# An encoder block on one core: row-summed modulation, gate A in the first stage, norms between units, y stored from ScalarE's queue

## The chip, the core and the metric

One core of a Trainium2 chip runs one launch. The metric is the device time in microseconds (us). Five engines work each in its own order: TensorE (PE: matmuls and transposes into PSUM banks), VectorE (DVE), ScalarE (ACT), GpSimd (POOL) and SyncE (SP, which here only issues DMAs). An instruction waits on semaphores for others; what stands behind it on its engine waits too. DMAs issued by SP or by ScalarE move data between HBM and SBUF.

## The reference

512 tokens, width 2048, float32. What matters here:

```python
c_act = silu(c)
mod = c_act @ w_ada + b_ada                    # w_ada is 2048 x 12288
sh1, sc1, g1, sh2, sc2, g2 = split(mod, 6)
h = rms_norm(x, norm1_w) * (1 + sc1) + sh1
qa, ka, va, qb, kb, vb, ga, gb = split(h @ w_in)   # 1024, 256, 256, 3 x 1024, 2 x 2048 columns
ya = global_gqa(rope(rms_norm(qa)), rope(rms_norm(ka)), va)     # 8 heads, 2 kv heads
yb = neighbourhood_attention(qb, kb, vb, rpb)                   # 8 heads
merged = sigmoid(ga) * (ya @ w_oa) + sigmoid(gb) * (yb @ w_ob)
x = x + g1 * (merged @ w_out)
h2 = rms_norm(x, norm2_w) * (1 + sc2) + sh2
x = x + g2 * ((silu(h2 @ w_gate) * (h2 @ w_up)) @ w_down)
out = rms_norm(x, final_w)
```

## The kernel before

Every product is done in three float32r matmuls: each operand is split into a high part (ScalarE, L114, `whi`, `h3h`) and a low part (L115, `wlo`, `h3l`; VectorE, or POOL where the helper gets `eng=G`), and `mm3` multiplies high by high, high by low, low by high. A *unit* is one weight tile of 128 x 1024 (512 KB): loaded by SP into a `raw` buffer (four of them), split into `whi` and `wlo` (three of each), and used by 24 matmuls of 512 columns.

The stages, in order of time:

- *First stage* (L299 to L396). x comes in as four token tiles; each gets its row scale, is scaled, and is transposed by TensorE into `xnT`. Then nine slices of k (one or two of the sixteen 128-wide parts of the width): `ada1` makes scale `s1` and shift `t1` for the slice, ScalarE makes h from `xnT` (L351), POOL splits h and all weights, and TensorE accumulates kv (all k in four `mm` banks), the first half of q and one of gate A's four groups (`g_acc`, 512 columns) in pieces that VectorE adds up (L391).
- *Modulation.* `ada_mod` loads rows of `w_ada` for a few columns, multiplies them by silu(c) of that row and adds them up over sixteen k on VectorE (`acc`, L255 and L257); TensorE sums over the partitions by a matmul against a column of ones (L275, bank `Y`, raised in priority), and VectorE finishes s and t (L263 to L265). `ada_gate` does the same for the gates g1 and g2.
- *Norm and attention A.* `norm_rope` (L422) norms and rotates k and then q (L450 to L455) and transposes them (L437); heads 0 to 3, q's second half (`form2`), gate A's rest (`gates`), q's second norm and heads 4 to 7 follow. `keep_y` (L463) stores each head's y to HBM by SP's queue.
- *Attention B* (L570 on): per half v, then per pair of heads q and k, then `att_b`. Behind each unit `pump` runs one step of the background list `bg`: scale and shift of the second norm, later the gates g1 and g2.
- *Gate B* (L583), then the loads and splits of y (L595), the merge (`w_oa`, `w_ob`), `w_out`, the feed-forward part and the last norm.

A scheduler sets each engine's order from the program, buffers and priorities; pools that are released give their space to the next, whose first writers wait for the old users.

Of the kernel before, what the change touches and what calls it, by code (L numbers as in the profile page):

```python
# [17 lines left out]
P = 128  # L18
D = 2048
# [61 lines left out]
def encoder_block(ctx: ExitStack, tc, xp, c, w_ada, b_ada, norm1_w, w_in, q_norm_w, k_norm_w, tb,  # L81
# [22 lines left out]
    const.tile([P, 32], F32, name="left_edge")  # L104
# [36 lines left out]
    later = []  # L141

# [28 lines left out]
    def form2(w, c0, xs, evac, r0=0, eng=V, tiles=range(NT)):  # L171

        n = len(xs)
        banks = {i: bank("mm") for i in tiles}
        for k0 in range(0, n, 2):
            m = min(2, n - k0)
            hi, lo = wsplit(w, r0 + k0, m, c0, 512, eng)
            for kk in range(m):
                xh, xl = xs[k0 + kk]
                for i in tiles:  # L180
                    sl = slice(i * P, (i + 1) * P)
                    mm3(banks[i], xh[:, sl], xl[:, sl], hi[:, kk], lo[:, kk], k0 + kk == 0, k0 + kk == n - 1)
            pump()
        for i in tiles:
            evac(i, banks[i])
# [24 lines left out]

    vrow = io.tile([P, 512], F32, tag="io", name="vrow")[:112, :P]
    row = lambda ap: ap.rearrange("o (k p) -> (o k) p", p=P)
    nc.scalar.dma_start(vrow[0:16], row(c))
# [15 lines left out]
    t2 = const.tile([P, KT], F32, name="t2")  # L229

    accp = io

    def ada_units(cols, w, pool=None):

        nj = len(cols)
        nk = 1024 // (nj * w)
        for k0 in range(0, KT, nk):
            raw = (pool or wp).tile([P, 1024], F32, tag="raw", name="raw", bufs=5 if pool else wbufs["raw"])
            r4 = raw.rearrange("p (k c n) -> p k c n", k=nk, c=nj)
            for j, col in enumerate(cols):  # L240
                src = w_ada[k0 * P:(k0 + nk) * P, col:col + w]
                nc.sync.dma_start(r4[:, :, j], src.rearrange("(k p) n -> p k n", p=P))
            yield [(k0 + e, raw[:, e * nj * w:(e + 1) * nj * w]) for e in range(nk)]

    def ada_acc(cols, w, bias, pool=None):


        acc = accp.tile([P, 512], F32, tag="acc", name="acc", bufs=2)[:, :len(cols) * w]
        if bias:
            G.memset(acc, 0.0)  # L250
            nc.sync.dma_start(acc[0:1, :], b_ada[:, cols[0]:cols[0] + w])
        for parts in ada_units(cols, w, pool):
            for k, part in parts:
                if k == 0 and not bias:
                    V.tensor_scalar(acc, part, cact[:, k:k + 1], None, op0=ALU.mult)  # L255
                else:
                    V.scalar_tensor_tensor(acc, part, cact[:, k:k + 1], acc, op0=ALU.mult, op1=ALU.add)  # L257
            yield None
        yield acc

    def ada_done(y, k0, n, s, b_s, nw, t, b_t):
        sl = slice(k0, k0 + n)
        V.tensor_add(s[:, sl], y[:, :n], b_s[:, sl])  # L263
        V.tensor_add(t[:, sl], y[:, n:2 * n], b_t[:, sl])
        V.scalar_tensor_tensor(s[:, sl], s[:, sl], 1.0, nw[:, sl], op0=ALU.add, op1=ALU.mult)  # L265

    def ada_mod(sh, sc, k0, n, to, pool=None):

        for acc in ada_acc((sc + k0 * P, sh + k0 * P), n * P, False, pool):
            if acc is None:  # L270
                yield
        with tc.high_priority():
            y = bank("Y")
            for j in range(2 * n):
                nc.tensor.matmul(y[:, j:j + 1], acc[:, j * P:(j + 1) * P], ones[:, 0:1], start=True, stop=True)  # L275
            ada_done(y, k0, n, *to)
        yield

    def ada_gate(col, q, dst):

        for acc in ada_acc((col + q * 512,), 512, True):
            if acc is None:
                yield
# [9 lines left out]

    def rows(dst, src):
# [4 lines left out]
    p_h = tc.alloc_tile_pool(name="p_h", bufs=1, side="left")  # L299
    xt = [[p_h.tile([P, 512], F32, tag=f"h{15 - 2 * i - q // 2}{'hl'[q % 2]}", name=f"xt{i}{q}") for q in range(4)]  # L300
          for i in range(NT)]
    p_q = tc.alloc_tile_pool(name="p_q", bufs=1, side="left")
# [3 lines left out]
    p_x = tc.alloc_tile_pool(name="p_x", bufs=1, side="right")  # L306
    g_acc = [p_x.tile([P, T], F32, name=f"g_acc{j}") for j in range(4)]
    xnT = p_x.tile([P, KT, T], F32, name="xnT")
    for i in range(NT):
        acc = small.tile([P, 4], F32, tag="acc4", name="acc4")  # L310
        bn = small.tile([P, 2, 6], F32, tag="bn", name="bn")
        mv = small.tile([P, 2], F32, tag="mv", name="mv")
        for q in range(4):
            nc.sync.dma_start(xt[i][q], xp[i * P:(i + 1) * P, q * 512:(q + 1) * 512])
            if q < 2:
                square(xt[i][q], acc[:, q:q + 1])
            else:
                V.bn_stats(bn[:, q - 2], xt[i][q])
        V.bn_aggr(mv, bn)
        V.tensor_mul(mv[:, 0:1], mv[:, 0:1], mv[:, 0:1])  # L320
        V.tensor_add(mv[:, 0:1], mv[:, 0:1], mv[:, 1:2])
        V.tensor_scalar(acc[:, 2:3], mv[:, 0:1], 1024.0, None, op0=ALU.mult)
        r = row_rstd(acc[:, :3])
        for q in range(4):
            V.tensor_scalar(xt[i][q], xt[i][q], r, None, op0=ALU.mult)
            tp = bank("S")
            for j in range(4):
                nc.tensor.transpose(tp[:, j * P:(j + 1) * P], xt[i][q][:, j * P:(j + 1) * P], ident)
            S.activation(xnT[:, 4 * q:4 * q + 4, i * P:(i + 1) * P], tp.rearrange("p (k t) -> p k t", k=4), AF.Copy)
    hT = [pair(p_h, f"h{k}", T, 1) for k in range(KT)]  # L330

    sg_a = [dram.tile([P, T], F32, name=f"sga{j}") for j in range(KT)]
    sg_b = [dram.tile([P, T], F32, name=f"sgb{j}") for j in range(KT)]
    kv_b = [bank("mm") for _ in range(NT)]
    turn = itertools.cycle("SST")
    slices = [(0, 1), (1, 2)] + [(k, k + 2) for k in range(2, KT, 2)]

    def ada1(k0, k1):  # L340
        to = (s1, b_sc1, n1, t1, b_sh1)
        for _ in ada_mod(0, D, k0, k1 - k0, to, p_x):
            pass

    ada1(*slices[0])
    for n, (k0, k1) in enumerate(slices):
        hp = tc.high_priority()
        hp.__enter__()
        for k in range(k0, k1):
            hf = io.tile([P, T], F32, tag="io", name="hf")  # L350
            S.activation(hf, xnT[:, k], AF.Identity, scale=s1[:, k:k + 1], bias=t1[:, k:k + 1])  # L351
            split(*hT[k], hf, G)
        hp.__exit__(None, None, None)
        ks = range(k0, k1)
        hi, lo = wsplit(w_in, k0, len(ks), KA, 512, G)
        for k in ks:
            for i in range(NT):
                sl = slice(i * P, (i + 1) * P)
                nc.tensor.matmul(kv_b[i], hT[k][0][:, sl], hi[:, k - k0], start=k == 0, stop=False)  # L359
                nc.tensor.matmul(kv_b[i], hT[k][0][:, sl], lo[:, k - k0], start=False, stop=False)  # L360
        for k in ks:
            for i in range(NT):
                sl = slice(i * P, (i + 1) * P)
                nc.tensor.matmul(kv_b[i], hT[k][1][:, sl], hi[:, k - k0], start=False, stop=k == KT - 1)
        if k1 == KT:
            kv = []
# [3 lines left out]
        for c0, accs, ends in ((QA, q_acc, (0, 1, 2, 4, 8, 12, 16)), (GA, g_acc, (0, 2, 6, 10, 14, 16))):  # L370
            if k1 not in ends:
                continue
            a0 = ends[ends.index(k1) - 1]
            ws = {}
            for k in range(a0, k1, 2):
                m = min(2, k1 - k)
                hi, lo = wsplit(w_in, k, m, c0, 512, G)
                ws.update({k + e: (hi[:, e], lo[:, e]) for e in range(m)})
            for i, acc in enumerate(accs):
                sl = slice(i * P, (i + 1) * P)  # L380
                b = bank(next(turn))
                for k in range(a0, k1):
                    (wh, wl), (hh, hl) = ws[k], hT[k]
                    if accs is q_acc:
                        mm3(b, hh[:, sl], hl[:, sl], wh, wl, k == a0, k == k1 - 1)
                    else:
                        mm3(b, wh[:, sl], wl[:, sl], hh, hl, k == a0, k == k1 - 1)
                if a0 == 0:
                    S.activation(acc, b, AF.Copy)
                else:  # L390
                    V.tensor_add(acc, acc, b)  # L391
        if n + 1 < len(slices):
            ada1(*slices[n + 1])
    for j in range(4):
        nc.sync.dma_start(sg_a[j], g_acc[j])
# [58 lines left out]
    for i, r in enumerate(rstds(q_acc, 4)):  # L454
# [518 lines left out]
```

## Time and profile before

| | |
|---|---|
| median of three runs | 2755.62 us (2755.6 to 2761.97) |
| profiled execution | 2758.62 us; its span 2756.6 us |
| TensorE busy | 2627.7 us, 95% of the span |
| VectorE, ScalarE, POOL busy | 1758.6, 961.2, 290.4 us |
| mean granted TensorE clock | 0.974 of full speed |
| moved by DMA | 427 MB, 155 GB/s in the mean |

A row of a stage table has the stretch (us from the span's start), its length, then for each engine the busy time and the number of instructions, the granted TensorE clock, the DMA engines' busy share and their GB/s. A row of one instruction group has line, engine, operation, output and inputs, shapes and count, then busy us and mean ns, then the engine's idle time ahead of it and what ended that. A row of the timeline begins with start and duration in us; an idle time ahead of it stands in square brackets with its releaser. PEld is TensorE's weight load, SPq and ACTq are DMA issues.

### The profile page before, as it was taken

To read this page: it belongs to the slowest core of one execution; us is meant where nothing else is said; L and a number is where in the kernel's file an instruction comes from. 1 tells how busy PE (TensorE), PEld (TensorE's weight loads), DVE (VectorE), ACT (ScalarE), POOL (GpSimd) and SP (SyncE) were. 2 spreads that over 40 slices of the span, in tenths; PEclk is the share of its full clock that TensorE was granted. 3 is DMA by queue.
4 is the path that set the end of the run, shared out by engine and by line. 5 is a ranking of instruction groups with operands and counts; after the bars stand their busy time and mean duration, and the time that the engine had idled before them with its cause. 6 is when DMAs were issued, how large, how long until landed. Compare 5 with 4: busy or idle time off the path is not lost.

```text
span 2756.6 us, 38761 instructions
## 1 busy us (share of the span) xinstructions
PE 2627.7 (95%) x15353; PEld 2298.7 (83%) x15353; DVE 1758.6 (64%) x2465; ACT 961.2 (35%) x1310; POOL 290.4 (11%) x178
## 2 busy tenths in 40 slices
PE   5888999999999999989979999999999999999998
PEld 4666878788887778867779999999999998878886
DVE  7886552466664566655567888888888873243227
ACT  4224532233331143322354444444444442222222
POOL 2444224000000000001110000000000000011001
PEclk8898999999999999999989999999999999999999
DMA  8772224655556677686533433443334455343332
GB/s 260 251 245 80 71 81 132 188 166 169 171 156 184 191 247 237 207 290 203 164 98 122 128 115 119 131 131 123 123 123 137 125 168 200 99 149 120 98 115 84
DMA packets 281237, 427.17 MB, mean 155 GB/s; under 512 B 16992, under 2 KB 148432, under 8 KB 278496
## 3 DMA queue, kind: packets, MB, share of 16 engines
q1 hardware_dynamic: 280720, 423.59, 48.8%
q8 instruction: 120, 1.97, 0.3%
q10 hardware_dynamic: 336, 1.11, 0.1%
q14 instruction: 61, 0.50, 0.1%
HBM read 392.11 MB, written 32.52 MB: 154 GB/s over the span
## 4 chain that ended last, share of the span: by engine, by line
PE 80%; DVE 8%; DMA 7%; issue 2%; ACT 2%; SPq 0%; POOL 0%; DVEq 0%; ACTq 0%
PE mm L122 20%; PE mm L124 20%; PE mm L123 20%; DMA raw<-in_w_ada 4%; DVE acc L257 4%; PE S L122 4%; PE S L123 4%; PE S L124 4%; PE Y L122 2%; PE Y L123 2%; PE Y L124 2%; DMA ffr<-ffd 1%; PE Y L275 1%; PE mm L359 1%; PE T L494 1%
## 5 line engine op out<-in xcount | busy, mean ns | idle before, releaser
L114 ACT ACTIVATE whi<-raw 128x1024 fp32r<-128x1024 f32 (+1 forms) x466 | 455.3, 979 | 1043.6 <-PE mm L124 394.2
L115 DVE TENSOR_TENSOR wlo<-raw,whi 128x1024 fp32r<-128x1024 f32 (+1 forms) x408 | 457.7, 1125 | 390.1 <-ACT whi L114 384.8
L257 DVE SCALAR_TENSOR_TENSOR acc<-raw,cact,acc 128x512 f32<-128x512 f32 (+1 forms) x383 | 318.0, 833 | 163.0 <-DMA raw<-in_w_ada 155.6
L646 POOL TENSOR_TENSOR xr<-xr,ro 128x512 f32<-128x512 f32 x32 | 49.1, 1563 | 1225.0 <-DVE ro L645 1225.0
L115 POOL TENSOR_TENSOR wlo<-raw,whi 128x1024 fp32r<-128x1024 f32 (+1 forms) x58 | 141.4, 2444 | 249.6 <-ACT whi L114 224.2
L115 DVE TENSOR_TENSOR wlo<-ta,whi 128x1024 fp32r<-128x1024 f32 x84 | 102.9, 1224 | 70.6 <-ACT whi L114 70.5
L114 ACT ACTIVATE whi<-ta 128x1024 fp32r<-128x1024 f32 x84 | 89.6, 1066 | 131.8 <-PE mm L123 131.8
L114 ACT ACTIVATE whi<-tb 128x1024 fp32r<-128x1024 f32 x84 | 89.7, 1067 | 124.1 <-PE S L123 122.1
L123 PE MATMUL mm<-x1l,whi 128*128 128x256 f32 x400 | 110.6, 276 | 0.0
L124 PE MATMUL mm<-x1h,wlo 128*128 128x256 f32 x400 | 110.6, 276 | 0.0
L122 PE MATMUL mm<-x1h,whi 128*128 128x256 f32 x400 | 110.5, 276 | 0.0
L115 DVE TENSOR_TENSOR wlo<-tb,whi 128x1024 fp32r<-128x1024 f32 x84 | 102.6, 1221 | 6.2 <-ACT whi L114 3.5
L122 PE MATMUL mm<-x0h,whi 128*128 128x256 f32 x368 | 102.8, 281 | 3.3 <-ACT whi L114 3.3
L124 PE MATMUL mm<-x0h,wlo 128*128 128x256 f32 x368 | 103.2, 280 | 0.8 <-DVE wlo L115 0.8
L123 PE MATMUL mm<-x0l,whi 128*128 128x256 f32 x368 | 103.0, 280 | 0.0
L124 PE MATMUL mm<-x2h,wlo 128*128 128x256 f32 x336 | 92.9, 276 | 0.0
L124 PE MATMUL mm<-x3h,wlo 128*128 128x256 f32 x336 | 92.9, 276 | 0.0
L124 PE MATMUL S<-x2h,wlo 128*128 128x256 f32 x336 | 92.9, 276 | 0.0
L123 PE MATMUL S<-x3l,whi 128*128 128x256 f32 x336 | 92.9, 276 | 0.0
L124 PE MATMUL Y<-x1h,wlo 128*128 128x256 f32 x336 | 92.9, 276 | 0.0
L124 PE MATMUL S<-x3h,wlo 128*128 128x256 f32 x336 | 92.9, 276 | 0.0
L123 PE MATMUL mm<-x3l,whi 128*128 128x256 f32 x336 | 92.9, 276 | 0.0
(1312 smaller groups left out, 8002.6 us busy)
## 6 DMA issues: line engine op xcount, KB each, us to landing
raw<-in_w_in SPq DMA_DIRECT2D x134, 512.0 KB
raw<-in_w_ada SPq DMA_DIRECT2D x256, 256.0 KB
raw<-in_w_gate SPq DMA_DIRECT2D x88, 512.0 KB
raw<-in_w_up SPq DMA_DIRECT2D x88, 512.0 KB
raw<-in_w_down SPq DMA_DIRECT2D x88, 512.0 KB
raw<-in_w_ada SPq DMA_DIRECT2D x64, 512.0 KB
raw<-in_w_out SPq DMA_DIRECT2D x40, 512.0 KB
ffr<-ffd SPq DMA_DIRECT2D x22, 512.0 KB
```

Source lines behind the costliest of these rows:

```text
L114: S.activation(hi, src, AF.Copy)
L115: eng.tensor_sub(lo, src, hi)
L122: nc.tensor.matmul(o, lh, rh, start=start, stop=False, **kw)
L123: nc.tensor.matmul(o, lh, rl, start=False, stop=False, **kw)
L124: nc.tensor.matmul(o, ll, rh, start=False, stop=stop, **kw)
L257: V.scalar_tensor_tensor(acc, part, cact[:, k:k + 1], acc, op0=ALU.mult, op1=ALU.add)
L275: nc.tensor.matmul(y[:, j:j + 1], acc[:, j * P:(j + 1) * P], ones[:, 0:1], start=True, stop=True)
L359: nc.tensor.matmul(kv_b[i], hT[k][0][:, sl], hi[:, k - k0], start=k == 0, stop=False)
L494: nc.tensor.transpose(tp[:, k * P:(k + 1) * P], e[:, k * P:(k + 1) * P], ident)
L646: eng.tensor_add(x2[i][:, cs], x2[i][:, cs], o)
```

## The change

- *Modulation by row sums.* The host now lays out the four shift and scale parts of `w_ada` transposed (`w_mod`: one row of 2048 per output). silu(c) is spread to all partitions once (`cb`), by four matmuls and ScalarE. For each 128-wide part k, four tiles of 128 x 1024 are loaded, and one VectorE instruction each multiplies by `cb` and writes the row's sum (`accum_out`); three tiny ones finish s and t. No matmul is left in it. The gates' columns stand in `w_gmod`, and `ada_gate` works as before.
- *First stage.* All four row scales come from one root; ScalarE and VectorE share the scaling. Per k TensorE transposes into bank `Y`, and h is made straight from there. All sixteen gate A groups (four of 512 columns) are in this stage, each in four pieces of four k. All splits are on VectorE; POOL has none. The sums for part k + 2 are asked for behind part k.
- *Norms.* k's and q's `norm_rope` steps, eight of them, are put in the list `between`, and `form2` runs one behind each unit of q's second half, which now stands ahead of attention A.
- *Gate B* moves into attention A's gaps (four column tiles, then eight); the last four stand behind attention B, where the loads of y are now written ahead of them with a buffer pair of their own.
- *y* is stored from ScalarE's queue.
- *Background list.* All 16 parts of the second modulation (two steps each, two tiles a step) and all gate steps are in it from attention B's start.

```diff
+    def ada_mod(m, k, cb, to, pool, tag, bufs):
+        s, b_s, nw, t, b_t = to
+        y = small.tile([P, 2, 2], F32, tag="mod", name="mod")
+        for j in range(2):
+            r0 = (2 * m + 1 - j) * D + k * P
+            for e in range(2):
+                es = slice(e * 1024, (e + 1) * 1024)
+                raw = pool.tile([P, 1024], F32, tag=tag, name="araw", bufs=bufs)
+                nc.sync.dma_start(raw, w_mod[r0:r0 + P, es])
+                V.scalar_tensor_tensor(raw, raw, 1.0, cb[:, es], op0=ALU.mult, op1=ALU.mult,
+                                       accum_out=y[:, e, j:j + 1])
+            if j == 0:
+                yield
...
-            split(*hT[k], hf, G)
+            split(*hT[k], hf)
...
-        for c0, accs, ends in ((QA, q_acc, (0, 1, 2, 4, 8, 12, 16)), (GA, g_acc, (0, 2, 6, 10, 14, 16))):
+    EARLY, LATE = (0, 1, 2, 4, 8, 12, 16), (0, 4, 8, 12, 16)
+        for c0, acc in accs.items():
+            ends = EARLY if c0 == QA else LATE
...
+                if k == KT - 1 and c0 in keep:
+                    nc.sync.dma_start(keep[c0][i], acc[i])
+        if k + 2 < KT:
+            ada1(k + 2)
...
-    for i, r in enumerate(rstds(kv, 2)):
-        norm_rope(kv[i], 2, i, r, nw["k"], kT)
+    rk, rq = rstds(kv, 2), rstds(q_acc, 4)
+    between.extend(functools.partial(norm_rope, kv[i], 2, i, rk[i], nw["k"], kT) for i in range(NT))
+    between.extend(functools.partial(norm_rope, q_acc[i], 4, i, rq[i], nw["q"], q) for i in range(NT))
+    form2(w_in, QA + 512, hT, lambda i, b: S.activation(q1[i], b, AF.Copy), eng=G)
...
-        nc.sync.dma_start(y_d[h], o)
+        nc.scalar.dma_start(y_d[h], o)
...
-    gates(sg_a, GA, 4, 8, G)
+    gates(sg_b, GB, 0, 4, G)
...
-    gates(sg_a, GA, 8, 16, G)
+    gates(sg_b, GB, 4, 12, G)
...
-    bg.extend(ada_mod(3 * D, 4 * D, k, 2, (s2, b_sc2, n2, t2, b_sh2)) for k in range(0, KT, 2))
+    bg.extend(ada_mod(1, k, cb, (s2, b_sc2, n2, t2, b_sh2), wp, "raw", 4) for k in range(KT))
+    bg.extend(ada_gate(0, q, g1_d) for q in range(4))
+    bg.extend(ada_gate(1, q, g2_d) for q in range(4))
...
+    p_y = tc.alloc_tile_pool(name="p_y", bufs=1, side="right")
+    for h in range(KT):
+        yr = p_y.tile([P, T], F32, tag="yr", name="yr", bufs=2)
+        nc.sync.dma_start(yr, y_d[h])
+        split(*yT[h], yr)
+    gates(sg_b, GB, 12, KT)
```

How the order moves, at three places. First VectorE in the first stage, about k = 1 to 3 (`s`, `t` are s1 and t1; `st` are q's accumulators). Before:

```order
L257 SCALAR_TENSOR_TENSOR acc<-raw,cact,acc 128x512
L263 TENSOR_TENSOR s_98<-Y,vec 128x1
L264 TENSOR_TENSOR t_99<-Y,vec 128x1
L257 SCALAR_TENSOR_TENSOR acc<-raw,cact,acc 128x512
L265 SCALAR_TENSOR_TENSOR s_98<-s_98,vec 128x1
L257 SCALAR_TENSOR_TENSOR acc<-raw,cact,acc 128x512 x8
L391 TENSOR_TENSOR st<-st,S 128x512
```

and now:

```order
L116 TENSOR_TENSOR h2l<-hf,h2h 128x512
L392 TENSOR_TENSOR st<-st,S 128x512
L392 TENSOR_TENSOR st<-st,T 128x512
L392 TENSOR_TENSOR st<-st,S 128x512 x2
L285 SCALAR_TENSOR_TENSOR araw,mod<-araw,cb 128x1024 x2
L116 TENSOR_TENSOR wlo<-raw,whi 128x1024
L291 TENSOR_TENSOR modz<-mod 128x2
L285 SCALAR_TENSOR_TENSOR araw,mod<-araw,cb 128x1024
L292 SCALAR_TENSOR_TENSOR s_113<-modz,vec 128x1
L293 TENSOR_TENSOR t_114<-modz,vec 128x1
```

The sums are half as many instructions per k and no longer read bank `Y`, and the splits of weights and of h have come onto VectorE between them.

Second TensorE at the norms, with `mm` the banks of q's second half and `rt` the rotated rows of k. Before:

```order
L124 MATMUL mm<-whi,h1l 128x512
L122 MATMUL mm<-whi,h2h 128x512
L437 MATMUL T<-ident,rt 128x128 x2
L123 MATMUL mm<-wlo,h2h 128x512
L124 MATMUL mm<-whi,h2l 128x512
```

and now:

```order
L123 MATMUL mm<-whi,h2h 128x512
L438 MATMUL T<-ident,rt 128x128 x2
L124 MATMUL mm<-wlo,h2h 128x512
L125 MATMUL mm<-whi,h2l 128x512
L123 MATMUL mm<-whi,h2h 128x512
```

The first transpose stood behind 25 matmuls of q's second half and stands behind 28 of them; the next ones stood 6 to 9 matmuls apart and stand a whole unit apart.

Third SP in attention B, where `raw<-in_w_in` are the projections' weights, `braw` the bias rows. Before:

```order
L531 DMA braw<-in_tb 8x720 x2
L129 DMA raw<-in_w_in 128x4x256
L531 DMA braw<-in_tb 8x720 x3
L466 DMA y_1973<-yo 128x512
L242 DMA raw<-in_w_ada 128x2x256 x2
```

and now:

```order
L403 DMA sgb_260<-go 128x512
L130 DMA raw<-in_w_in 128x2x512
L284 DMA araw<-in_w_mod 128x1024 x2
L130 DMA raw<-in_w_in 128x2x512
L284 DMA araw<-in_w_mod 128x1024 x2
L531 DMA braw<-in_tb 8x720
```

Two loads of 256 KB into one buffer behind each weight tile have become two of 512 KB into two buffers, and the stores of y have left this queue.

More of the change, by code (lines that the diff above doesn't have):

```diff
@@ L229, in encoder_block @@
     t2 = const.tile([P, KT], F32, name="t2")
+    for b_s in (b_sc1, b_sc2):
+        V.tensor_scalar(b_s, b_s, 1.0, None, op0=ALU.add)
     accp = io
[L233 to L283, printed above, removed]
+    def ada_gate(g, q, dst):
+        acc = accp.tile([P, 512], F32, tag="acc", name="acc", bufs=2)
+        G.memset(acc, 0.0)
+        col = (2 + 3 * g) * D + q * 512
+        nc.sync.dma_start(acc[0:1, :], b_ada[:, col:col + 512])
+        for k0 in range(0, KT, 2):
+            _, r3 = unit(w_gmod, k0, 2, g * D + q * 512, 512)
+            for e in range(2):
+                V.scalar_tensor_tensor(acc, r3[:, e], cact[:, k0 + e:k0 + e + 1], acc, op0=ALU.mult, op1=ALU.add)
+            yield
@@ L315, in encoder_block @@
             if q < 2:
-                square(xt[i][q], acc[:, q:q + 1])
+                square(xt[i][q], sq[:, i, q:q + 1])
             else:
                 V.bn_stats(bn[:, q - 2], xt[i][q])
[L319 to L329, printed above, removed]
@@ L330, in encoder_block @@
-    hT = [pair(p_h, f"h{k}", T, 1) for k in range(KT)]
+        V.bn_aggr(mv[:, i], bn)
+    V.tensor_mul(ssq4, mv[:, :, 0], mv[:, :, 0])
+    V.tensor_add(ssq4, ssq4, mv[:, :, 1])
+    V.scalar_tensor_tensor(ssq4, ssq4, 1024.0, sq[:, :, 0], op0=ALU.mult, op1=ALU.add)
+    V.tensor_add(ssq4, ssq4, sq[:, :, 1])
+    r4 = rsqrt_mean(ssq4, D, NT)
+    for q in range(4):
+        for i in range(NT):
+            if q == 0 or i % 2:
+                S.activation(xt[i][q], xt[i][q], AF.Copy, scale=r4[:, i:i + 1])
+            else:
+                V.tensor_scalar(xt[i][q], xt[i][q], r4[:, i:i + 1], None, op0=ALU.mult)
@@ new lines, in h_tile @@
+    def h_tile(k):
+        with tc.high_priority():
+            tp = bank("Y")
+            for i in range(NT):
+                nc.tensor.transpose(tp[:, i * P:(i + 1) * P], xt[i][k // 4][:, k % 4 * P:(k % 4 + 1) * P], ident)
+            hf = io.tile([P, T], F32, tag="io", name="hf")
+            S.activation(hf, tp, AF.Identity, scale=s1[:, k:k + 1], bias=t1[:, k:k + 1])
+            hT.append(pair(p_h, f"h{k}", T, 1))
+            split(*hT[k], hf)
+    kv = []
+    for k in range(KT):
+        if k % 2 == 0:
+            whi, wlo = wsplit(w_in, k, 2, KA, 512)
+        if k == 0:
+            ada1(0)
+            ada1(1)
+        h_tile(k)
+        for i in range(NT):
+            sl = slice(i * P, (i + 1) * P)
+            mm3(kv_b[i], hT[k][0][:, sl], hT[k][1][:, sl], whi[:, k % 2], wlo[:, k % 2], k == 0, k == KT - 1)
+        if k == KT - 1:
@@ L592, in encoder_block @@
     mT = [pair(p_m, f"m{k}", T, 1) for k in range(KT)]
-    p_y = tc.alloc_tile_pool(name="p_y", bufs=1, side="right")
-    yT = [pair(p_y, f"y{k}", T, 1) for k in range(KT)]
-    for h in range(KT):
-        yr = wp.tile([P, 1024], F32, tag="raw", name="yr", bufs=4)[:, :T]
-        nc.sync.dma_start(yr, y_d[h])
-        split(*yT[h], yr)
     def gated(src, dst):
```

123 lines of the change are left out of this document (61 added, 62 removed).

## The prediction

> **What bounds the kernel now.** I read the page first, then a table of stages, then TensorE's waits stage by stage, and last single rows of time for prices.
>
> ```profile
> span 2756.6 us, 38761 instructions
> ...
> PE 2627.7 (95%) x15353; PEld 2298.7 (83%) x15353; DVE 1758.6 (64%) x2465; ACT 961.2 (35%) x1310; POOL 290.4 (11%) x178
> ...
> PE   5888999999999999989979999999999999999998
> ...
> PEclk8898999999999999999989999999999999999999
> ```
>
> TensorE (PE) is busy 95% of the span, so only its idle time and its slow-clock time can be won. Both lie at the left edge: the first slices (69 us each) show 5, 8, 8, 8 tenths at a clock of 0.8 to 0.9. The stages:
>
> ```profile
> core 0: us, PE busy (x) PEld busy (x) DVE busy (x) ACT busy (x) POOL busy (x), PEclk, DMA share, GB/s
> 0.00:228.00 228.00, 175.88 (x706) 140.33 (x707) 184.19 (x286) 81.40 (x164) 93.28 (x50) 0.88 0.73 234
> 228.00:270.00 42.00, 33.29 (x132) 25.79 (x131) 32.42 (x71) 11.76 (x20) 18.81 (x12) 0.84 0.30 97
> 270.00:500.00 230.00, 225.34 (x1123) 182.34 (x1123) 104.88 (x218) 86.65 (x175) 70.59 (x33) 0.99 0.33 103
> 500.00:850.00 350.00, 345.66 (x1625) 284.20 (x1624) 211.00 (x387) 106.17 (x183) 20.14 (x21) 1.00 0.56 169
> 850.00:1010.00 160.00, 150.87 (x640) 123.37 (x639) 82.16 (x105) 37.72 (x43) 1.51 (x3) 0.95 0.64 196
> 1010.00:1200.00 190.00, 180.40 (x774) 146.96 (x773) 121.11 (x159) 63.21 (x84) 1.58 (x3) 0.97 0.74 241
> ```
>
> These are the first stage, the k and q norm, attention A with gates, attention B, gate B's tail, and the start of the merge. Busy time hides the slow clock, so I price TensorE's work by its warm pitch:
>
> ```profile
> 206.79 0.63 PE L359 MATMUL mm<-whi,h14h 128*128 128x512 f32 x1
> 207.22 0.63 PE L360 MATMUL mm<-wlo,h14h 128*128 128x512 f32 x1
> ...
> 213.38 0.39 PE L122 MATMUL S<-whi,h14h 128*128 128x512 f32 x1
> ...
> 227.66 0.39 PE L124 MATMUL S<-h15h,wlo 128*128 128x512 f32 x1
> ```
>
> Between the last two rows lie 63 starts in 14.28 us: 0.227 us for a 512-column matmul. The first two, soon after a wait, stand 0.43 us apart: each wait costs itself and some us of half speed behind it. The first stage's 576 projection matmuls (16 k, 12 each for kv, q and one gate group) are 131 us warm; it takes 228. Who makes it wait (total, times, longest):
>
> ```profile
> PE Y L275 <- DVE acc L257: 16.8, 6, 5.0
> ...
> PE S L328 <- DVE xt L325: 14.1, 3, 6.4
> ...
> PE T L437 <- DVE rt L434: 3.5, 1, 3.5
> ...
> SPq L242 <- DVE acc L257: 81.1, 44, 5.3
> ...
> L257 DVE SCALAR_TENSOR_TENSOR acc<-raw,cact,acc 128x512 f32<-128x512 f32 x105 | 114.1, 1087 | 2.9
> ...
> L257 DVE SCALAR_TENSOR_TENSOR acc<-raw,cact,acc 128x512 f32<-128x512 f32 x90 | 68.8, 764 | 40.3 <-DMA raw<-in_w_ada 39.0
> ...
> 21.96 0.48 DVE L257 SCALAR_TENSOR_TENSOR acc<-raw,cact,acc 128x256 f32<-128x256 f32 x1
> ...
> L115 DVE TENSOR_TENSOR wlo<-raw,whi 128x1024 fp32r<-128x1024 f32 x55 | 69.1, 1256 | 60.1 <-ACT whi L114 58.4 <-DMA y<-yo 1.3 <-DMA raw<-in_w_ada 0.4
> ```
>
> VectorE (DVE) bounds the first stage: it is busy 184 of 228 us, TensorE waits for its accumulator, and even the load queue waits 81 us for it. The first L257 row is from 40 to 203 us, while POOL splits weights (POOL busy 93 us): 1087 ns. The second is from attention B, with POOL nearly idle: 764 ns.
>
> **The change, part by part.** All against the profiled execution's 2758.6 us; the median shown, 2755.6, is 3.0 lower.
>
> *A, first stage.* Removed: 128 accumulating L257 passes with their column-sum matmuls, and all of POOL's splits. Added: 64 row-summing passes over 128x1024, and twelve more gate groups (576 matmuls, 131 us warm) that before stood behind this stage. Price of the new pass, which no row shows: 256 to 512 columns adds 0.28 us (0.48 to 0.764), so 1024 costs about 1.33; twice 764 is 1.53; a read-out of the sum may add some 0.2 (ScalarE has one, below). Ends 1.33 and 1.73; I take 1.5, between the two extrapolations and a small read-out. The contended 2 x 1087 = 2.17 is not an end for the likeliest case, since POOL has no work there.
>
> ```profile
> 18.27 0.69 DVE L318 BATCH_NORM_STATS2 bn<-xt 128x6 f32<-128x512 f32 x1
> ...
> 21.83 0.15 DVE L198 TENSOR_TENSOR rr<-rr,rt 128x1 f32<-128x1 f32 x1
> ...
> 30.63 1.66 DVE L325 TENSOR_SCALAR xt<-xt,rr 128x512 f32<-128x512 f32 x4
> ...
> L391 DVE TENSOR_TENSOR st<-st,S 128x512 f32<-128x512 f32 x11 | 7.4, 681 | 1.2 <-PE S L124 1.2
> ...
> 258.45 0.60 PE L437 MATMUL T<-ident,rt 128*128 128x128 f32 x4
> ```
>
> The start: x is read by 18.3 us and the last row scale is there at 21.8; the one root for all four token tiles comes as late, say 22. Until the first gate group may start (k = 0 to 3 done) VectorE has in its queue 20 row sums (five k, 30 us), 6 scalings at 0.42 (2.5), 4 full and 2 half weight splits (6.4), 4 h splits (2.8), 4 q additions (2.7) and some 15 tiny ones (2.3): 47 us. The q additions stand ahead of k = 3's sums and wait for TensorE's k = 1, some 5 us. So the gate groups start at about 74 us. From there TensorE has 1056 matmuls (240 us), 36 transposes at about 0.115 (4) and 2 us of cold clock. VectorE's remaining 44 sums, 45 splits, 64 additions and 12 h splits are about 175 us, 70% of that time, so it no longer paces. But at each of 16 group edges the second weight tile gets its buffer only six matmuls (1.4 us) ahead of its use, while ScalarE and VectorE need some 2.3 us for the split: between 0 and 2 us each, I take 0.7 (11). End at 74 + 240 + 4 + 2 + 11 = 331, against 227.9 + 131 = 359 before for the same work: **28 us won**.
>
> *B, k's and q's norm between units.* From 228 to 270 TensorE ran 24 transposes and 108 matmuls, 27 us warm in 42: 15 lost.
>
> ```profile
> 234.95 0.61 DVE L430 SCALAR_TENSOR_TENSOR rt<-st,rr,nwk 128x128 f32<-128x128 f32 x2 [5.38 <-DMA sga<-g_acc]
> ...
> 237.20 0.69 PE L437 MATMUL T<-ident,rt 128*128 128x128 f32 x2 [3.49 <-DVE rt L434]
> ```
>
> The norm waited until gate A's stores had left the pool that it reuses, and its transpose came 9.5 us behind the last gate matmul. The changed kernel has that wait too: sixteen stores instead of four, the last queued behind a weight load. Its first transpose stands 28 matmuls (6.4 us) behind the gates; if the chain again takes 8.7 to 9.5, TensorE waits 2 to 3 us and runs 2 us cold. The later ones stand a whole unit (5.4 us) apart, and are covered. Loss 5 instead of 15: **10 won**.
>
> *C, column sums gone from attention B and gate B.*
>
> ```profile
> 517.41 1.02 PE L275 MATMUL Y<-ones,acc 128*128 128x1 f32 x8 [2.94 <-DVE acc L257]
> ...
> 864.37 1.74 PE L275 MATMUL Y<-ones,acc 128*128 128x1 f32 x8 [2.49 <-DVE acc L257]
> ...
> 920.12 1.02 PE L275 MATMUL Y<-ones,acc 128*128 128x1 f32 x8 [2.44 <-DVE acc L257]
> ...
> 999.64 0.77 PE L122 MATMUL mm<-y0h,whi 128*128 128x512 f32 x1 [4.19 <-issue]
> ```
>
> In 850 to 1010 us 624 matmuls are 141.6 warm, so 18 are lost: the last row with its cold matmuls is 6, the two L275 rows the other 12. With the one at 517, 17 us. Row sums need no TensorE: **17 won**.
>
> *D, the same sums as load and as VectorE work.* A unit of attention B (24 matmuls, 5.44 us) before carried one modulation tile of 512 KB beside its weight tile; now it carries two, for 32 units, out of the same four buffers: 1.57 MB per unit, 289 GB/s, where 170 flowed. VectorE: 64 x 1.5 + 32 x 1.25 + 42 for four heads and the v splits (211 us in the 500 to 850 row less 69 for L257 and 69 for weights leaves 73 for eight heads) = 178, against 174 + 18 = 192 for TensorE. Covered on average, but at 93%, and in order. Ends: 0, and 1.1 us a unit (35) if loads flow only at the 241 GB/s of the 1010 to 1200 row. I take **10 lost**, nearer to zero, since this chip gave far more where buffers were free:
>
> ```profile
> 12.00:16.00 4.00, 2.80 (x13) 2.43 (x14) 3.92 (x17) 3.12 (x9) 0.00 (x0) 1.00 1.04 395
> ...
> 0.73 0.42 ACTq L213 DMA_DIRECT2D vrow<-in_c  x1
> ...
> L475 ACT ACTIVATION_READ_ACCUMULATOR e<-S,mx 128x1 f32 x31 | 6.3, 204 | 0.0
> ```
>
> *E, y.* Loads of y now stand among gate B's last units, and the merge's first weights ahead of most of them: of the 6 us at 999.64 I count **4 won** (ends 6, and -4 if the last pair comes late: two buffers, and gate stores ahead of it). Stores of y cost ScalarE 0.42 each, 7 us in all; it is busy 87 of 230 us in attention A, so they are hidden, and exponentials wait 0.4 us at most. SP's queue is freed from waiting for them: nothing counted. Gate loads move from late stages into earlier ones; their bytes stay: nothing.
>
> Sum: 28 + 10 + 17 - 10 + 4 = 49. 2758.6 - 49 = 2709.6, and by the median **2707**.
>
> [...]
>
> **Rivals.** *The row sum takes twice the time* (2 x 1.33 = 2.7 us). Then the start grows by 20 x 1.2 = 24 and attention B, with VectorE at its limit, by 64 x 1.2 = 77: 2707 + 101 = 2808, slower. It decides from 1.5 + 49/84 = 2.1 us. For it: no row has this form, and the contended row reaches 2.17. Against: two fp32 inputs alone cost 764. *Three tiles a unit are too many for four buffers*: 35 instead of 10 in D, 2732. For it: 241 GB/s at four buffers and PE waits there. *All edges fit*: neither A's 11 nor D's 10 is paid, 2686. *The first stage stays paced by VectorE*, its in-order queue stalling on loads and on TensorE: A gains nothing, and with the second rival in D the whole is 2707 + 28 + 25 = 2760, no change.
>
> **Chances.** Forecast 52% (2690 to 2724), two times 10%, four buffers 19%, all edges fit 12%, no change 7%. The range 2682 to 2745 takes in the forecast, four buffers and most of the edges. By over 0.3% (8 us, about what a measurement can tell from no change) faster: forecast, four buffers and all edges, 0.83; within it 0.07; slower 0.10.
>
> **What will show it.** Row sums near 1.5 us on VectorE, and 178 us for 64 of them with their company in attention B; the first gate-group matmul near 74 us; the first stage's end near 331; no L275 on TensorE; the first norm transpose waiting 2 to 3 us; DMA near 290 GB/s in attention B with TensorE's clock at 1.00. It is wrong if the new pass is beyond 2 us, or if TensorE waits for weights in attention B.

## The result, and the profile after

The changed kernel takes 2724.5 us in the median of four runs (2717.8 to 2728.5) against 2755.6 for the kernel before (2752.5 to 2762.0): ratio 0.9882, 95% interval 0.9853 to 0.9910. That is 31 us, where 49 were forecast; between the profiled executions (2758.6 and 2721.3) it is 37. The head of the page after:

```profile
span 2719.5 us, 38209 instructions
...
PE 2594.8 (95%) x15233; PEld 2268.2 (83%) x15233; DVE 1735.6 (64%) x2517; ACT 969.6 (36%) x1315; POOL 202.1 (7%) x136
...
PE   5999999998989999999889999999999999999998
...
PEclk9999999998999999999989999999999999999999
...
L285 DVE SCALAR_TENSOR_TENSOR araw<-araw,cb 128x1024 f32<-128x1024 f32 x128 | 157.9, 1241 | 74.0 <-DMA araw<-in_w_mod 73.7
```

The left edge is filled: 5, 9, 9, 9 tenths where 5, 8, 8, 8 stood, at a clock of 0.9 from the first slice. New dents stand at slices 10 and 12 (a slice is 68 us). The last row is the new row sum: 1.24 us, and ahead of it VectorE stood idle for 74 us in all, waiting for modulation tiles. The stages of after (first stage with all of gate A; norms; attention A and, behind 510 us, most of gate B; first part of attention B; its rest with gate B's end; merge):

```profile
core 0: us, PE busy (x) PEld busy (x) DVE busy (x) ACT busy (x) POOL busy (x), PEclk, DMA share, GB/s
0.00:317.00 317.00, 285.67 (x1225) 227.22 (x1226) 203.05 (x353) 113.10 (x192) 4.21 (x10) 0.99 0.67 222
317.00:374.00 57.00, 48.95 (x215) 38.97 (x214) 40.43 (x60) 15.22 (x27) 30.55 (x17) 0.94 0.27 79
374.00:586.00 212.00, 206.79 (x1052) 169.06 (x1052) 107.84 (x237) 83.85 (x168) 61.23 (x29) 0.99 0.35 111
586.00:810.00 224.00, 200.01 (x891) 162.37 (x890) 154.45 (x306) 59.50 (x100) 9.06 (x9) 0.95 0.70 224
810.00:957.00 147.00, 146.81 (x692) 120.69 (x692) 98.31 (x182) 53.90 (x95) 11.87 (x13) 1.00 0.60 188
957.00:1147.00 190.00, 179.13 (x778) 147.06 (x776) 124.37 (x164) 67.56 (x91) 2.57 (x5) 0.98 0.68 220
```

The fourth row is where the change lost: TensorE busy 200 of 224 us at 0.95, VectorE only 154 of 224, and DMA at 224 GB/s, not 290. TensorE at the places that the terms rest on:

```profile
67.55 0.39 PE L123 MATMUL S<-h0h,whi 128*128 128x512 f32 x1
...
328.80 0.66 PE L438 MATMUL T<-ident,rt 128*128 128x128 f32 x2 [5.22 <-DVE rt L435]
...
631.10 0.80 PE L123 MATMUL mm<-h0h,whi 128*128 128x512 f32 x1 [10.26 <-DVE vl L116]
...
683.89 0.58 PE L124 MATMUL S<-qkl,qkh 128*128 128x256 f32 x1 [5.46 <-DVE qkl L116]
...
802.62 0.50 PE L123 MATMUL mm<-h0h,whi 128*128 128x512 f32 x1 [3.63 <-DVE vl L116]
...
957.15 0.39 PE L123 MATMUL mm<-y0h,whi 128*128 128x512 f32 x1
...
1078.78 0.79 PE L262 MATMUL Y<-ada_s,ones_r 128*128 128x512 f32 x1 [4.17 <-DVE ada_s L116]
```

To compare stretches that hold different work I take *loss*: length less the stretch's matmuls at the prediction's warm pitch (0.227 us for 512 columns, and so on). The one-column matmuls of the column sums (L275), which only the kernel before has, count as loss. Loss takes in the slow matmuls behind a wait: behind the one that ends at 631.10 us they start 0.43 us apart up to 636.4, at a clock of 0.50 from 631 to 636. The borders are events: the last gate A matmul of the first stage, the last matmul of attention A's eighth head, the merge's first (y0h), w_out's first.

| | before: loss, us | after: loss, us | won | forecast |
|---|---|---|---|---|
| first stage | 90.7 | 46.6 | 44 | 28 (A) |
| norms, attention A | 28.6 | 23.3 | 5 | 10 (B) |
| attention B, gate B, y's loads | 35.4 | 38.3 | -3 | 17 - 10 + 4 = 11 (C, D, E) |
| merge | 8.5 | 14.6 | -6 | 0 |
| w_out and the rest (length) | 1572.6 | 1571.8 | 1 | 0 |

Each loss is good to about 1 us. The sum is 41, 4 more than the spans show: the trace after holds twelve more matmul rows of 512 columns in the first four stretches, 2.7 us of work, eight of which spread silu(c) in the first 16 us; the rest is within that.

Beside the experiments about one execution in four, of the kernel before too, took some 30 us longer than the others, so the intervals of their ratios are wide and every one of them takes in 0.9882, and I read medians and, above all, where in the trace the loss lies.

### The profile page after: what moved, and what is told of

It is laid out like the page before. It is cut to its first block, busy times and chain, and to the rows that moved or that the text cites. A ratio compares the mean times of both kernels' runs of the same rounds, so it can differ in the third digit from the quotient of the medians.

```text
span 2719.5 us, 38209 instructions
## 1 busy us (share of the span) xinstructions
PE 2594.8 (95%) x15233; PEld 2268.2 (83%) x15233; DVE 1735.6 (64%) x2517; ACT 969.6 (36%) x1315; POOL 202.1 (7%) x136
## 4 chain that ended last, share of the span: by engine, by line
PE 76%; DMA 12%; DVE 8%; issue 2%; ACT 2%; SPq 0%; POOL 0%; DVEq 0%; ACTq 0%; POOLq 0%
PE mm L123 18%; PE mm L124 18%; PE mm L125 18%; DMA araw<-in_w_mod 5%; PE S L124 5%; PE S L123 5%; PE S L125 5%; DMA raw<-in_w_gmod 2%; PE Y L123 2%; PE Y L124 2%; PE Y L125 2%; DVE araw L285 2%; DMA ffr<-ffd 1%; DVE wlo L116 1%; DMA yr<-y 1%
## 5 line engine op out<-in xcount | busy, mean ns | idle before, releaser
L115 ACT ACTIVATE whi<-raw 128x1024 fp32r<-128x1024 f32 x465 | 455.7, 981 | 980.5 <-PE mm L125 387.1
L116 DVE TENSOR_TENSOR wlo<-raw,whi 128x1024 fp32r<-128x1024 f32 (+1 forms) x433 | 488.8, 1132 | 413.1 <-ACT whi L115 412.2
L285 DVE SCALAR_TENSOR_TENSOR araw<-araw,cb 128x1024 f32<-128x1024 f32 x128 | 157.9, 1241 | 74.0 <-DMA araw<-in_w_mod 73.7
L256 DVE SCALAR_TENSOR_TENSOR acc<-raw,cact,acc 128x512 f32<-128x512 f32 x128 | 96.5, 754 | 61.5 <-DMA raw<-in_w_gmod 59.7
L116 POOL TENSOR_TENSOR wlo<-raw,whi 128x1024 fp32r<-128x1024 f32 x32 | 77.7, 2431 | 436.7 <-ACT whi L115 418.0
L123 PE MATMUL mm<-x3h,whi 128*128 128x256 f32 x336 | 92.7, 276 | 0.0
L123 PE MATMUL mm<-x2h,whi 128*128 128x256 f32 x336 | 92.7, 276 | 0.0
L124 PE MATMUL mm<-x2l,whi 128*128 128x256 f32 x336 | 92.7, 276 | 0.0
```

The costliest lines, as they stand in the source:

```text
L115: S.activation(hi, src, AF.Copy)
L116: eng.tensor_sub(lo, src, hi)
L123: nc.tensor.matmul(o, lh, rh, start=start, stop=False, **kw)
L124: nc.tensor.matmul(o, lh, rl, start=False, stop=False, **kw)
L256: V.scalar_tensor_tensor(acc, r3[:, e], cact[:, k0 + e:k0 + e + 1], acc, op0=ALU.mult, op1=ALU.add)
L285: V.scalar_tensor_tensor(raw, raw, 1.0, cb[:, es], op0=ALU.mult, op1=ALU.mult, accum_out=y[:, e, j:j + 1])
```

## The experiments

The theory after the trace: modulation tiles come late out of four buffers that weights share (L), VectorE takes its work in order, and what TensorE needs stands behind them. The rival: it is VectorE's added work (W). VectorE in the first half of v, up to the end of TensorE's wait at 631 us:

```profile
585.70 1.22 DVE L116 TENSOR_TENSOR wlo<-raw,whi 128x1024 fp32r<-128x1024 f32 x1
...
623.61 1.22 DVE L116 TENSOR_TENSOR wlo<-raw,whi 128x1024 fp32r<-128x1024 f32 x1
627.49 1.23 DVE L285 SCALAR_TENSOR_TENSOR araw<-araw,cb 128x1024 f32<-128x1024 f32 x1 [2.66 <-DMA araw<-in_w_mod]
628.64 0.08 DVE L285 DVE_READ_ACCUMULATOR araw<-araw,cb 128x1 f32 x1
629.20 1.23 DVE L285 SCALAR_TENSOR_TENSOR araw<-araw,cb 128x1024 f32<-128x1024 f32 x1 [0.48 <-DMA araw<-in_w_mod]
630.35 0.08 DVE L285 DVE_READ_ACCUMULATOR araw<-araw,cb 128x1 f32 x1
630.35 2.48 DVE L116 TENSOR_TENSOR vl<-mm,vh 128x512 fp32r<-128x512 f32 x4
```

The two weight splits lie six units apart: 6.32 us a unit instead of 5.44, which is 1.57 MB at 249 GB/s. v's split (`vl`), which frees the banks that TensorE wants, stands behind two sums that wait for their loads.

How far such readings carry: five of the runs below (gate results by ScalarE alone, both runs on the first stage, norms ahead, y from SP's queue) leave the second modulation as it is. Their traces lose 35 to 40 us in attention B, and the first wait for v's split is 3.9 to 10.2 us. A difference within that shows nothing.

**Loads without sums.**

```diff
-                V.scalar_tensor_tensor(raw, raw, 1.0, cb[:, es], ...)
+                n = 1024 if m == 0 else 8
+                V.scalar_tensor_tensor(raw[:, :n], raw[:, :n], 1.0, cb[:, e * 1024:e * 1024 + n], ...)
```

(`m` is 1 for the second modulation.)

> In the second modulation (attention B) each row sum covers 8 columns of its tile instead of 1024; all 64 loads stay, and s2 and t2 are not the reference's. Theory L (the loads: VectorE stands in order behind modulation tiles that four buffers let through late, and v's and the weights' splits stand behind it): nearly nothing comes back, within 8 us of the changed kernel's 2724, and TensorE still waits some 10 us for v's split at 631 us and loses over 30 us between 586 and 928 us. Theory W (VectorE's work, 64 x 1.31 = 84 us): 20 to 27 us come back, 2697 to 2705.

Measured 2713.4 us (ratio 0.9829, 0.9753 to 0.9905). v's split in this kernel:

```profile
630.89 0.17 DVE L286 SCALAR_TENSOR_TENSOR araw<-araw,cb 128x8 f32<-128x8 f32 x1 [1.90 <-DMA araw<-in_w_mod]
630.98 0.08 DVE L286 DVE_READ_ACCUMULATOR araw<-araw,cb 128x1 f32 x1
630.98 2.48 DVE L116 TENSOR_TENSOR vl<-mm,vh 128x512 fp32r<-128x512 f32 x4
...
631.72 0.79 PE L123 MATMUL mm<-h0h,whi 128*128 128x512 f32 x1 [3.24 <-DVE vl L116]
```

Between the two theories, in the time too: L allowed 2716 to 2732, W 2697 to 2705. With eight columns left of each sum the split still waits for a modulation load. That it waits 3.24 us instead of 10.26 is little beyond what the unchanged runs show, but the loss in attention B, 31.5 instead of 38.3, is. Of the 26 us that the second modulation cost there (D, below) about 19 stay with the loads and 7 go with the sums, as far as one trace tells.

**Sums without loads.**

```diff
-                V.scalar_tensor_tensor(raw, raw, 1.0, cb[:, es], ...)
+                src, dst = (raw, raw) if m == 0 else (cb[:, es], pool)
+                V.scalar_tensor_tensor(dst, src, 1.0, cb[:, es], ...)
```

(For `m` = 1 the tile and its load are left out, and `pool` is one tile, `junk`.)

> The 64 row sums of the second modulation read silu(c)'s tile twice instead of a loaded tile; their loads (33.5 MB) are left out, and s2 and t2 are not the reference's. Theory L: 25 us or more come back, about 2695 to 2700, and the loss between 586 and 928 us falls from 38 to about 12 or less. Theory W: it stays within 8 us of 2724.

Measured 2722.2 us (0.989, 0.9785 to 0.9996): a miss for L, and the time that W gave. The waits at 631 and 684 us are gone, but others stand ahead of attention B:

```profile
603.10 1.22 DVE L287 SCALAR_TENSOR_TENSOR junk<-cb 128x1024 f32<-128x1024 f32 x1
604.25 0.08 DVE L287 DVE_READ_ACCUMULATOR junk<-cb 128x1 f32 x1
604.25 0.69 DVE L404 COPY go<-mm 128x512 f32<-128x512 f32 x1
...
595.62 0.79 PE L124 MATMUL mm<-wlo,h0h 128*128 128x512 f32 x1 [9.04 <-DVE wlo L116]
...
604.99 0.79 PE L123 MATMUL mm<-whi,h0h 128*128 128x512 f32 x1 [6.87 <-DVE go L404]
```

With no load to wait for, the scheduler put the sums in a row ahead of a weight split and of gate B's results (`go`, which leave by VectorE), and TensorE waited for these; attention B loses 36 us. So this run doesn't weigh VectorE's work in the same order; it shows that without a single late load the place of the sums in VectorE's order can cost as much.

**Two buffers of its own.** `wp, "raw", 4` becomes `p_b, "araw2", 2` in the background list.

> The second modulation's tiles get two buffers of their own beside the four that weights use. Theory L with the number of buffers as its cause (the prediction's second rival): the load rate between 586 and 810 us rises from 224 to over 270 GB/s and 15 to 25 us come back, 2700 to 2710. Theory L with the rate of the transfers themselves or SP's order as its cause: the rate stays below 245 GB/s and the time within 8 us of 2724. Theory W: within 8 us of 2724 too.

Measured 2723.7 us (0.9864, 0.9772 to 0.9957). The rate from 586 to 810 us, 206 GB/s, says little, since the sums now begin earlier; the pace of the units tells:

```profile
592.40 1.28 DVE L402 COPY go<-mm 128x512 f32<-128x512 f32 x2
...
601.44 1.23 DVE L116 TENSOR_TENSOR wlo<-raw,whi 128x1024 fp32r<-128x1024 f32 x1 [0.72 <-ACT whi L115]
...
606.88 1.23 DVE L116 TENSOR_TENSOR wlo<-raw,whi 128x1024 fp32r<-128x1024 f32 x1 [0.88 <-ACT whi L115]
...
612.32 1.23 DVE L116 TENSOR_TENSOR wlo<-raw,whi 128x1024 fp32r<-128x1024 f32 x1 [0.37 <-ACT whi L115]
...
593.14 0.79 PE L123 MATMUL mm<-whi,h0h 128*128 128x512 f32 x1 [7.62 <-DVE go L402]
...
797.90 0.80 PE L123 MATMUL mm<-h0h,whi 128*128 128x512 f32 x1 [5.46 <-DVE vl L116]
...
600.00:618.00 18.00, 18.00 (x81) 14.92 (x80) 11.42 (x22) 4.25 (x4) 0.00 (x0) 1.00 0.82 257
```

From 600 to 618 us, with two modulation tiles to each weight tile, TensorE is never idle and two units in a row take its 5.44 us; from 586 to 600 us 293 GB/s flowed. So the 249 GB/s of the changed kernel were the limit of four buffers there, not of the DMA engines. That no wait stands at 631 us says less: the sums have moved forward, and VectorE has none between 623 and 639 us. The time stayed, because the sums now stand ahead of `go` (10.9 us with the cold matmuls behind it) and v's second split still waits; attention B loses 36 us, as the unchanged runs do.

**Two buffers of its own, gate results by ScalarE.** The edit above, and in `keep_gate` `S.activation(o, b, AF.Copy)` for `V.tensor_copy(o, b)`.

> The two buffers of its own for the second modulation, plus gate B's results leaving their bank by ScalarE. Theory: with the two buffers the units run at TensorE's pace (5.44 us), and what is left is VectorE's order, of which the wait for gate results ahead of attention B (10.9 us with its cold matmuls) is taken away by the second edit: first matmul of the merge at about 945 us instead of 955, 2712 to 2716 in all. Rival, that the next item in VectorE's queue takes the wait over: 955 and 2724.

Measured 2720.1 us (0.9867, 0.9811 to 0.9923), the merge's first matmul at 951.9, attention B's loss 28.2: the wait for `go` is gone, a weight split's (4.09 us at 586) and v's second split's (5.07 at 795) are left. About halfway between theory and rival.

**One tile a step, from attention A on.**

```diff
-            if j == 0:
-                yield
+                if j == 0 or e == 0:
+                    yield
```

and the second modulation is put in the background list ahead of attention A's first head.

> The second modulation starts behind attention A's fourth head, where gate B's units leave the load queue at half rate, and takes one tile a step (64 steps) instead of two (32). Theory L: attention B's loss falls from 38 to about 12, and attention A gives back at most 5, since two tiles a unit are 512 + 512 KB in 5.4 us, 193 GB/s, beside a VectorE that is half idle there: 2700 to 2708. Theory W: the same sums run in the same time spread wider, so 2705 to 2715. A rival to both, that every modulation tile costs TensorE some 0.4 us wherever it stands: 2720 to 2728.

Measured 2724.2 us (0.987, 0.9795 to 0.9945). Attention B's loss fell to 16.4 as L has it, but attention A's rose from 23.3 to 38.0, not by the 5 that I allowed: sums stand between the exponentials' steps there (a transpose waits 2.48 us for a maximum). Another 8 us were lost behind w_out's start, where more of the gates' steps now run; up to 5 of it is what traces differ by there. The time is that of the third rival, a fixed price for each tile wherever it stands, and this run doesn't exclude it.

**One tile a step, from gate B's middle on; gate results by ScalarE.** The same, but put in the list only ahead of the eight gate column tiles that the program has between attention A and attention B.

> The second modulation with one tile a step, listed from the eight gate column tiles ahead of attention B on, so that 64 steps end with attention B; gate results leave by ScalarE; still four buffers. Theory: at two tiles a unit (193 GB/s) four buffers are enough, and attention A is left as it was: attention B and gate B lose 13 us instead of 38, first matmul of the merge at 930 to 938 us, some 4 us given back in w_out, where the gates' steps now stand: 2700 to 2712 in all. Rival: four buffers stay one load late at this rate too, and v's split waits 10 us as before: 945 to 957, 2716 to 2726.

Measured 2710.5 us (0.9841, 0.9785 to 0.9896; the changed kernel had 0.9882): the lowest median, 14 us under the changed kernel's, though the intervals overlap. From the first stage's end its stages are attention A (to 521), attention B (to 945) and the merge:

```profile
320.00:521.00 201.00, 185.09 (x950) 149.46 (x950) 136.32 (x283) 87.24 (x187) 68.73 (x34) 0.97 0.31 98
521.00:945.00 424.00, 412.81 (x1895) 339.12 (x1894) 239.01 (x453) 131.69 (x217) 50.21 (x33) 0.99 0.61 187
945.00:1130.00 185.00, 176.76 (x777) 145.21 (x775) 122.90 (x164) 67.10 (x91) 2.58 (x5) 1.00 0.69 224
...
633.43 0.79 PE L123 MATMUL mm<-h0h,whi 128*128 128x512 f32 x1 [5.96 <-DVE vl L116]
```

Attention B loses 20.4 us instead of 38.3, attention A 27.0, the merge 9.1 instead of 14.6. A and B together lose 47 instead of 62, so a tile does not cost the same wherever it stands. Not all is cured: the merge begins at 945 us, where L gave 930 to 938 and the rival 945 to 957, and v's split still waits 5.96 us. Two things besides the pace differ: gate results leave by ScalarE, and the gates' steps come later (16 of their 128 accumulations before the merge instead of 48). No run parts their shares.

**Gate results by ScalarE, the gates' partition-sum matmul a step later** (a `yield` behind `split(hi, lo, acc)`).

> Gate B's results leave their bank by ScalarE instead of VectorE, and the partition-sum matmul of the gates g1 and g2 comes one background step behind its split. Theory Q (VectorE's order: what TensorE waits for stands behind row sums or accumulations in VectorE's queue): the merge's two waits for the gate's split (8.5 us with the cold matmuls behind them) go, and attention B stays as it is, since no gate result was waited for there: 2714 to 2718 against 2724. Rival, that a wait that is removed is taken over by the next instruction in VectorE's queue: within 4 us of 2724.

Measured 2730.8 us (0.9859, 0.9785 to 0.9934). The merge's waits for the gate's split are gone, and its loss rose from 14.6 to 17.6: TensorE waits instead for gated products that VectorE writes late (3.36 us at 1122.6). The wait was taken over, as the rival has it, though the time lies 3 us above the rival's too; the first stage, which the edit leaves alone, lost 3 us more in this trace. Attention B stays as it is, with 10.18 us of waiting for v's split.

**Both lists together** (one tile a step from attention A on, and the two edits of the run before).

> The second modulation from attention A on with one tile a step, plus both edits of the run before. Theory Q: the first matmul of the merge at about 945 us (950 with the early list alone, less the 4.8 lost on a gate result), w_out's first at about 1128, and 2704 to 2712 in all. Rival: later stages give it back, because the 144 background steps now end in w_out and behind it: 2716 to 2724.

Measured 2733.7 us (2721.1 to 2755.6; 0.9883, 0.9791 to 0.9974). Attention A loses 39.2, attention B 21.9, with 10.42 us of waiting for v's split, and the merge begins at 960 us instead of 945. A miss for the theory, and the rival's reason isn't seen either: w_out and the rest take 1571.6 us, as in the changed kernel. What makes v's split late here, and not with the early list alone, is the order on VectorE again: one sum that waits for its load (4.71 us) stands directly ahead of it.

**The first stage's sums twice.** Behind each row sum of the first stage a second one of the same tile.

> Each row sum of the first stage is done twice (64 more passes of 1.31 us, 84 us of VectorE work; s1 and t1 are not the reference's). The prediction's step for the first stage (VectorE paces only the start, 20 sums; afterwards it has slack): first gate-group matmul at 68 + 26 = 94 us, first stage's end at 317 + 26 to 35, time 2750 to 2760. Rival (VectorE paces the whole stage): the end at 390 to 400 us, time 2795 to 2808.

Measured 2741.1 us in the median of eight (0.9933, 0.9879 to 0.9987). VectorE and TensorE, up to the first gate group and from there to the stage's end:

```profile
0.00:87.00 87.00, 44.67 (x130) 29.11 (x131) 74.81 (x151) 33.22 (x56) 1.64 (x8) 0.88 0.76 257
87.00:331.00 244.00, 243.93 (x1095) 201.36 (x1094) 197.13 (x331) 79.94 (x136) 2.40 (x1) 1.00 0.62 197
...
86.95 0.39 PE L123 MATMUL S<-h0h,whi 128*128 128x512 f32 x1
```

The first gate group starts 19.4 us later, for 20 added sums of 1.31 us (26); the stage ends at 331.5, 14.4 later, though 64 sums (84 us) were added. Both are below the theory's own 94 and 343 to 352, and far from the rival's 390: VectorE paces the start, and mostly nothing behind it.

**Splits of the first stage on POOL** (`eng=G` for its weights and h, as before the change).

> All splits of the first stage go back to POOL. Theory (two engines on SBUF slow each other, as the accumulating passes of before with 1087 against 764 ns suggest): row sums of 1.7 to 2.2 us instead of 1.24 while POOL splits, POOL's own splits 2.4 us or more instead of 1.25, and the first stage's end later than 317 us by 10 to 40. Rival (POOL takes the splits off VectorE for nothing): row sums stay at 1.24 and the end is at 300 to 317 us.

One execution: 2763.6 us, the stage's end at 358.0. VectorE's and POOL's groups within the stage:

```profile
L116 POOL TENSOR_TENSOR wlo<-raw,whi 128x1024 fp32r<-128x1024 f32 x42 | 108.6, 2601 | 144.4 <-ACT whi L115 144.4
L285 DVE SCALAR_TENSOR_TENSOR araw<-araw,cb 128x1024 f32<-128x1024 f32 x64 | 98.9, 1569 | 34.7 <-DMA araw<-in_w_mod 34.6
...
160.27 1.22 DVE L285 SCALAR_TENSOR_TENSOR araw<-araw,cb 128x1024 f32<-128x1024 f32 x1
...
160.80 6.28 POOL L116 TENSOR_TENSOR wlo<-raw,whi 128x1024 fp32r<-128x1024 f32 x2 [7.84 <-ACT whi L115]
...
164.75 3.41 DVE L285 SCALAR_TENSOR_TENSOR araw<-araw,cb 128x1024 f32<-128x1024 f32 x1
```

and in the changed kernel, in the same stretch:

```profile
L285 DVE SCALAR_TENSOR_TENSOR araw<-araw,cb 128x1024 f32<-128x1024 f32 x64 | 77.5, 1223 | 17.2 <-DMA araw<-in_w_mod 17.1
L116 DVE TENSOR_TENSOR wlo<-raw,whi 128x1024 fp32r<-128x1024 f32 x47 | 57.3, 1223 | 35.7 <-ACT whi L115 35.7
```

The mean of 1569 ns is below the theory's 1.7 us, but it mixes two kinds: a sum that starts ahead of POOL's splits takes 1.22 us, one beside them 3.41. With the splits on POOL the stage ends 41 us later, nearly all that it had gained: the row sums alone did not win the stage; that VectorE takes the splits as well did its part.

**Norms ahead of q's second half** (called at once instead of put in `between`).

> k's and q's norm steps stand ahead of q's second half in the program instead of between its units. The prediction's step for the norms (the transposes then have nothing to cover them): the loss between 317 and 374 us grows from 11 to about 20 us, 2732 to 2736. Rival: the scheduler by itself puts matmuls of q's second half ahead of transposes that are not ready, and the place in the program hardly matters: within 4 us of 2724.

Measured 2728.6 us (0.9858, 0.977 to 0.9946); loss up to attention A's end 27.5 instead of 23.3. The first transpose waits the same 5.0 us, a later one 2.66. The place in the program is worth 4 us of the 9 that the step expected; the scheduler by itself does the rest.

**y stored from SP's queue.**

> y is stored from SP's queue again. The prediction's step (the stores are hidden in either queue): the loss between 374 and 586 us stays at 12 us within 2, and the merge begins at 957 within 4. Rival (SP's loads queue behind stores that wait for ScalarE): the loss grows by more than 4 us.

One execution, 2729.7 us. The loss of norms and attention A is 23.6 (23.3), as the prediction's step has it; the merge begins at 962.6 instead of 957.2, 3.2 of it lost already at the first stage's end, which this edit doesn't touch. So the bound of 4 us on the merge is missed, but not by the stores: hidden in either queue, within what one execution tells.

## Why the prediction was nearly right, term by term

The median, 2724.5 us, lies at the upper edge of the forecast's 2690 to 2724 and nearer to the second rival's 2732 than to 2707. Of the prediction's two signs of being wrong, the new pass stayed short, and TensorE did wait in attention B, though less for weights (1.24 us at most) than for the splits of v, q and k.

**The price of the row sum** was just below its lower end: 1.22 and 0.09 us for the read-out in the first stage, 1.31 against 1.5 taken and 1.33 as the lower bound. The rival of twice the time fell: the sum takes 1.22 us, and a plain subtraction of the same shape 1.22 too.

**A** had the right mechanism, and was sized some 14 us too low: the stage ends at 317 us instead of 331 (16 by the table, which counts the eight matmuls that spread silu(c) as work). The start was 6.5 us earlier (67.55 against 74); 20 sums at 0.19 less are 3.8 of it, and the doubled sums show that the start goes with VectorE. The step that failed is "at each of 16 group edges ... I take 0.7 (11)": from the first gate group to the stage's end there are 249.5 us for 244 of work, so edges and cold clock together cost 5.5 instead of 13.

**B** won 4 instead of 10 in the norms' own stretch: 317 to 374 us lose 11 where 5 were forecast, against 15 before. The first transpose waited 5.22 us, not 2 to 3, and a later one 1.93 at 354.6, which the prediction held to be covered. Attention A behind it loses about what it did (12 against 13). The interleaving itself is worth 4.

**C** came as forecast: no L275 wait is left on TensorE. It counted three of the eight groups of column sums in attention B; the other five, which waited for next to nothing, took TensorE 0.8 us each, some 4 us more that the change saves.

**D** is where the prediction was most wrong. "I take **10 lost**, nearer to zero, since this chip gave far more where buffers were free": it lost some 26 (38.3 against 35.4 less 17 for C and 6 for y's transition), or 30 with C's other 4. The row at 395 GB/s was no measure for a stretch where buffers are not free; the second rival's 241 GB/s was, with 249 measured. That rival's price of 35 was nearer than 10, and the run with two buffers more, where 293 GB/s flowed, agrees with its cause. But the buffers are not the whole, for with them the loss stayed. D asked whether VectorE's work fits (178 of 192 us), when what counted was which piece stands ahead of which: VectorE was busy 69% while TensorE waited for it.

**E**: the transition into the merge no longer costs anything, 6 us won instead of 4 (957.15 has no wait). The merge itself lost 6 more. The prediction put the earlier gate steps at nothing, and two waits for their split (1.57 us at 975, 4.17 at 1079) are about that size; but with these waits gone the loss was 17.6, and with one tile a step 9.1. What exactly makes it 14.6 stays open.

So 49 became 31 to 37: A gave some 15 more, D took 16 more, B and the merge took 6 each, E gave 2. That the errors of A and D cancel is luck; neither size was foreseen.

## What to carry to other kernels

Background work on an in-order engine is priced by what stands behind it when its load is late, not by its busy share: attention B lost 16 to 22 us at one tile a unit and 38 at two, though at one tile a part of the tiles, and of the gates' steps, ran in other stretches. When a buffer pool is shared, work out the rate that its buffers sustain from a stretch where they were all in use; here a peak from a stretch with free buffers (395 GB/s) misled. And a gain measured at one wait must be followed to the next item in the same queue: four of these runs took a wait away and got little or nothing, since another took its place.

## What was unexpected of the hardware

A 128x1024 float32 pass that multiplies two SBUF tiles and sums each row costs 1.22 us and 0.09 for the read-out; a plain subtraction of the same shape costs 1.22 too. With the first stage's splits on POOL it took 1.57 us in the mean over that stage and 3.41 beside two of POOL's splits, and POOL's split of the same shape took 2.60 us in the mean against VectorE's 1.22.
